# Dilated attention scores in 256-column products, taken 6 ticks later

## The chip, the cores and the metric

The kernel runs on one core of one Trainium2 chip. The metric is the device time of one execution in microseconds (us). Engines are named as in the profile: PE is TensorE (PEld its weight loads), DVE is VectorE, ACT is ScalarE, POOL is GpSimd, SP issues most of the DMAs.

## The reference

An encoder trunk of two layers over 512 tokens of 1024 features, in float32. Layer 0 is a gated linear recurrence, layer 1 is dilated sliding-window attention; each is followed by a gated feed-forward block with a width-3 convolution, with LayerNorms between. Only the scores of the attention are touched. There are 16 heads of 64 features and three groups of (window, dilation): (128, 1), (512, 4), (2048, 16). For each group, with keys gathered by stride:

```
s = einsum(q, k) * Dh**-0.5 - slope[h] * |distance|   # masked outside the window
p = exp(s - max(s));  o = einsum(p, v) / sum(p)
```

and the outputs of the three groups are merged by their softmax denominators, then projected by `w_o`.

## The kernel before, in words

**Products.** A float32 product is made from parts: each operand x is split into a rounded high part (ACT copies it to the type float32r) and the rest x - high (DVE subtracts), and a projection is three PE passes, high*high, high*low and low*high, accumulated in PSUM (`passes`, L216 to L219). Projection weights come by DMA as 128x1024 tiles (`wraw`), are split two units ahead of their use (ACT L156 makes `whi`, DVE L159 makes `wlo`), and are loaded four ahead.

**Order.** Everything is emitted in an order written out by the program; each engine then runs its own instructions in that order and waits by semaphores. The clock of that order is the *tick*: in a unit of a q or k projection (`cols_unit`, L278) one tick follows each of 8 steps of three 512-column matmuls; in a unit of the v projection (`v_unit`, L998) one follows every two steps, six 256-column matmuls. At a tick one item may be taken from two queues, `scores` first, then `values`, and the next one no sooner than `GAP` = 2 ticks later (L266 to L276). So the items of attention stand singly between blocks of projection matmuls.

**Attention.** `ORDER` (L688) runs through four blocks: q and k of head pairs p = 2c and p = 2c+1 (for each group g = 0, 1, 2 one q unit and one k unit, 48 ticks a pair), then v of both pairs (48 ticks). After each q or k unit `evac` (L761) takes the result out of PSUM. For keys it makes, for each of the two heads h of the pair, a high part `ka[:, h]` and a low part `kl[:, h]` on 64 partitions (ACT L785, DVE L789), and copies each by a DMA on SP to the other 64 partitions (L787, L791). The query tile holds q's high part on the head's 64 partitions and its low part on the other 64. So one matmul of the query tile with `ka[:, h]`, over all 128 partitions, gives q times the high keys, and one with `kl[:, h]` adds q times the low keys.

After the k unit of a group `push_scores` (L857) puts the scores of its two heads in the queue, to be taken no sooner than `SLAG` = 10 ticks later (for p = 0 by `XLAG`: 10, 11 and 14). Group 0 is four items `score0` (L808), each with four matmuls of 256 columns (two runs of 128 keys); groups 1 and 2 are two items each, `score12` (L833): for each of four classes r of tokens two matmuls of 128 columns into one PSUM bank, with `ka` and then with `kl` on top, L840 and L841; then one DVE instruction adds the distance bias over 512 columns, L842. With the last head of group 2 the softmax parts are joined by `merge` (L874): small steps at 8 to 28 ticks after, and from `T0` = 56 ticks after, the items of `values`: `pv_turn` (four transposes of the probabilities, L946, split by ACT L389 and DVE L390) and, at least `LAG` = 9 ticks behind its turn, `pv_prod` (L971, L974).

**End of the stage.** After the last v unit the output projection begins (L1084 on): one tick after every job of three matmuls, items of `values` at every tick, then the LayerNorm.

**Room.** PSUM is 8 banks and SBUF 40 slots of 4 KB per partition, both given out first-freed-first by `Arena` (L35); whoever takes one waits for its last user.

Of the kernel before, what the change touches and what calls it, by code (L numbers as in the profile page):

```python
# [11 lines left out]
F32R = mybir.dt.float32r  # L12
I32 = mybir.dt.int32
AF = mybir.ActivationFunctionType
OP = mybir.AluOpType
# [10 lines left out]


GAP, GAP_WO = 2, 1
SLAG, XLAG = 10, (10, 11, 14)
LAG, LAG_WO, VLAG, OLAG, T0 = 9, 4, 10, 4, 56  # L30
DEEP = 3
WIDE = 1
# [24 lines left out]
def encoder(ctx: ExitStack, tc: tile.TileContext, x, ln_g, ln_b, rg_w_in, rg_conv_w, rg_conv_b,  # L57
            rg_w_a, rg_b_a, rg_w_x, rg_b_x, rg_lam, rg_w_out, at_w_qkv, at_w_o, ff_w_up,
            ff_conv_w, ff_conv_b, ff_w_down, out):
    nc = tc.nc  # L60
# [14 lines left out]
    sb = Arena(ctx.enter_context(tc.tile_pool(name="slots", bufs=1)), NSLOT, "s")  # L75
    small = ctx.enter_context(tc.tile_pool(name="small", bufs=2))
    ps = Arena(ctx.enter_context(tc.tile_pool(name="ps", bufs=1, space=bass.MemoryType.PSUM)), 8, "b")
    ctx.enter_context(tc.manual_schedule())

    def bank(name):  # L80
        return ps.get([128, 512], F32, name)
# [4 lines left out]
    def f(ap):  # L86
        return ap.bitcast(F32)
# [662 lines left out]
    def attention(i0, d0, d12):  # L750
        slopes = [2.0 ** (-8.0 * (h + 1) / H) for h in range(H)]
        qk, P0, P12, V = {}, {}, {}, {}
        o32, ohl = {}, {}
        stats = {}
        def cls(b, lo=0, hi=128):

            return b[lo:hi].rearrange("p (j r) -> p r j", r=4)
# [3 lines left out]
        def evac(p, g, which, b):  # L761
            if which == "q":
                qa = sb.get([128, 2, 512], F32R, "q")
                if g == 0:
                    src = lambda lo, hi: b[lo:hi].rearrange("p (n i r) -> p n r i", n=4, r=4)
                    dst = lambda h, lo, hi: qa[lo:hi, h].rearrange("p (n r i) -> p n r i", n=4, r=4)
                else:
                    src = lambda lo, hi: cls(b, lo, hi)
                    dst = lambda h, lo, hi: qa[lo:hi, h].rearrange("p (r j) -> p r j", r=4)
                for h, a, z, o, oz in halves:  # L770
                    nc.scalar.activation(dst(h, a, z), src(a, z), AF.Copy)
                for h, a, z, o, oz in halves:
                    nc.vector.tensor_tensor(dst(h, o, oz), src(a, z), f(dst(h, a, z)), OP.subtract)
                qk[p, g, "q"] = qa
            else:
                ka = sb.get([128, 2, 512], F32R, "k")
                kl = sb.get([128, 2, 512], F32R, "kl")
                if g == 0:
                    src = lambda lo, hi: b[lo:hi]
                    dst = lambda t, lo, hi: t[lo:hi]  # L780
                else:
                    src = lambda lo, hi: cls(b, lo, hi)
                    dst = lambda t, lo, hi: t[lo:hi].rearrange("p (r j) -> p r j", r=4)
                for h, a, z, o, oz in halves:
                    nc.scalar.activation(dst(ka[:, h], a, z), src(a, z), AF.Copy)  # L785
                for h, a, z, o, oz in halves:
                    nc.sync.dma_start(f(ka[o:oz, h]), f(ka[a:z, h]))  # L787
                for h, a, z, o, oz in halves:
                    nc.vector.tensor_tensor(dst(kl[:, h], a, z), src(a, z), f(dst(ka[:, h], a, z)), OP.subtract)  # L789
                for h, a, z, o, oz in halves:  # L790
                    nc.sync.dma_start(f(kl[o:oz, h]), f(kl[a:z, h]))  # L791
                qk[p, g, "k"] = (ka, kl)
            ps.put(b)

        scores, values = deque(), deque()
# [6 lines left out]
        def keys(t, lo, hi, blk):  # L802

            st = {0: (0, 64), 3: (320, 64)}.get(blk, (128 * blk - 64, 128))
            s = t[lo:hi]
            return bass.AP(tensor=s.tensor, offset=s.offset + st[0], ap=[list(s.ap[0]), [st[1], 2], [1, 128]])

        def score0(p, h, half):  # L808
            qa, (ka, kl) = qk[p, 0, "q"], qk[p, 0, "k"]
            sl = -8.0 * slopes[2 * p + h]  # L810
            if half == 0:
                if h == 0:
                    stats[p] = small.tile([128, 2, 2, 2, 4], F32, name="stats", bufs=2)
                P0[p, h] = sb.get([128, 4, 256], F32, "P0")
            b = bank("s0")
            for z in range(2):
                blk = 2 * half + z
                o = b[:, 256 * z:256 * z + 256].rearrange("p (a c) -> p a c", a=2)
                js = slice(128 * blk, 128 * blk + 128)
                nc.tensor.matmul(o, qa[:, h, js], keys(ka[:, h], 0, 128, blk), start=True, stop=False)  # L820
                nc.tensor.matmul(o, qa[:, h, js], keys(kl[:, h], 0, 128, blk), start=False, stop=True)
            for z in range(2):
                blk = 2 * half + z
                nc.vector.scalar_tensor_tensor(
                    P0[p, h][:, blk, :], d0[:, (0, 1, 1, 2)[blk], :], sl, b[:, 256 * z:256 * z + 256],
                    op0=OP.mult, op1=OP.add)
            ps.put(b)
            if half:
                softmax(p, h, 0, P0[p, h])
                if h:  # L830
                    drop(p, 0)

        def score12(p, h, g):  # L833
            qa, (ka, kl) = qk[p, g, "q"], qk[p, g, "k"]
            if g == 1:
                P12[p, h] = sb.get([128, 4, 2, 128], F32, "P12")
            b = bank("s12")
            for r in range(4):
                c = slice(128 * r, 128 * r + 128)
                nc.tensor.matmul(b[:, c], qa[:, h, c], ka[:, h, c], start=True, stop=False)  # L840
                nc.tensor.matmul(b[:, c], qa[:, h, c], kl[:, h, c], start=False, stop=True)  # L841
            nc.vector.scalar_tensor_tensor(  # L842
                P12[p, h][:, :, g - 1, :], d12[:, g - 1:g, :].to_broadcast([128, 4, 128]), -8.0 * slopes[2 * p + h],
                b.rearrange("p (r c) -> p r c", r=4), op0=OP.mult, op1=OP.add)
            ps.put(b)
            if g == 2:
                softmax(p, h, 1, P12[p, h].rearrange("p r g c -> p r (g c)"))
            if h:
                drop(p, g)
                if g == 2:  # L850
                    merge(p)

        def drop(p, g):
            for t in (qk.pop((p, g, "q")),) + qk.pop((p, g, "k")):
                sb.put(t)

        def push_scores(p, g):  # L857
            ready = after(XLAG[g] if p == 0 else SLAG)
            for h in range(2):
                if g == 0:  # L860
                    for half in range(2):
                        scores.append((ready, lambda h=h, half=half: score0(p, h, half)))
                else:
                    scores.append((ready, lambda h=h: score12(p, h, g)))

        def softmax(p, h, w, P):
            st = stats[p]
            nc.vector.tensor_reduce(st[:, w, 0, h, :], P, axis=AX.X, op=OP.max, negate=True)
            nc.vector.tensor_scalar(st[:, w, 0, h, :], st[:, w, 0, h, :], 0.125, None, op0=OP.mult)  # L869
            for b in range(4):  # L870
                nc.scalar.activation(P[:, b, :], P[:, b, :], AF.Exp, bias=st[:, w, 0, h, b:b + 1], scale=0.125,  # L871
                                     accum_out=st[:, w, 1, h, b:b + 1])
# [172 lines left out]
        for kind, n in ORDER:  # L1045
            for g in (range(3) if kind == "qk" else VG):
                if kind == "qk":
                    for which in "qk":
                        if n == 0 and g < 2:
                            if g == 0 and which == "q":  # L1050
                                fb = first_units(i, 4, ["q", "k", "q", "k"])
                                wrap()
                            b = fb.pop(0)
                        else:
                            b = bank("qk")
                            cols_unit(b, i)
                        evac(n, g, which, b)
                        i += 1
                    push_scores(n, g)
                else:  # L1060
                    while values and values[0][2] // 2 < n:
                        tick()
                    if n:
                        for z in range(2):
                            sb.put(V[g, z])
                    v_unit(n, g, i)
                    i += 2
                    if g == VG[-1]:
                        vdone[0] = n
                        vtime[0] = clock[0] + VLAG  # L1070
# [21 lines left out]
        while left or at_k.get(KD - 1, BIG) > clock[0]:  # L1092
# [9 lines left out]
            if job:  # L1102
                h, k, t = job
# [53 lines left out]
    d0, d12 = dist  # L1157
# [31 lines left out]
```

## Time and profile before

| | |
|---|---|
| Time, median of 3 runs | 1565.41 us (1564.68 to 1566.1) |
| The profiled execution's own time | 1563.55 us |
| its span, first to last instruction | 1561.8 us |
| PE busy | 1528.5 us (98%) |
| PEld busy | 1314.0 us (84%) |
| DVE busy | 920.1 us (59%) |
| ACT busy | 662.2 us (42%) |
| POOL busy | 145.8 us (9%) |
| mean granted TensorE clock | 0.996 |

Busy is the time in which at least one instruction of the engine was under way; PE's ends are modelled and its matmuls overlap, so PE's pace is read from the starts of its instructions. The chain of waits goes back from the last instruction, at each step to what released it. All times inside the execution are us from the span's start; the attention stage lies between about 612 and 1177 us.

### The profile page before, as it was taken

The page shows a single profiled execution, that of the slowest core. Times are in us where ns is not written, and L with a number is a line of the kernel's source. Part 1 is how long each engine was busy: PE and PEld are TensorE (multiplying, and loading weights), DVE is VectorE, ACT ScalarE, POOL GpSimd, SP SyncE. Part 2 cuts the span into 40 slices and gives each one's busy share as a digit, 9 for nine tenths or more (in the row PEclk, how much of TensorE's full clock was granted, in tenths as well). Part 3 has the DMA queues.
Part 4 walks back from the last instruction along what each step waited for, and adds up shares of the span by engine and source line. Part 5 has one row for each costly group of instructions (what it writes and reads, how often), then busy time and mean ns, then how long its engine had stood idle before and what let it go on. Part 6 is the DMA issues. An engine that isn't in the chain of part 4 may idle for free.

```text
span 1561.8 us, 20972 instructions
## 1 busy us (share of the span) xinstructions
PE 1528.5 (98%) x8115; PEld 1314.0 (84%) x8115; DVE 920.1 (59%) x1314; ACT 662.2 (42%) x1062; POOL 145.8 (9%) x367
## 2 busy tenths in 40 slices
PE   7899999999999999999999999999999999999998
PEld 6678889888888888979889889988988888888886
DVE  5688786564544245685677668568657445454225
ACT  3678942333333211554455455355542433333210
POOL 2211002000000002022012001101202000000001
PEclk9999999999999999999999999999999999999999
DMA  5956643222323331335343343433434222323311
GB/s 174 202 131 131 207 147 95 81 82 83 89 85 121 121 108 54 85 106 162 82 116 123 100 122 103 141 94 110 148 115 129 82 81 87 88 81 108 135 68 54
DMA packets 228752, 173.04 MB, mean 111 GB/s; under 512 B 17294, under 2 KB 205996, under 8 KB 228652
## 3 DMA queue, kind: packets, MB, share of 16 engines
q1 hardware_dynamic: 210860, 159.11, 33.8%
q0 software_dynamic: 17792, 12.58, 3.7%
q8 instruction: 64, 1.05, 0.3%
q14 instruction: 36, 0.29, 0.1%
HBM read 145.44 MB, written 2.10 MB: 94 GB/s over the span
## 4 chain that ended last, share of the span: by engine, by line
PE 90%; DVE 4%; DMA 2%; ACT 2%; issue 1%; POOL 1%; SPq 0%; DVEq 0%; ACTq 0%; POOLq 0%
PE v L218 24%; PE o L218 20%; PE g L218 15%; PE qk L218 15%; PE gate L218 2%; PE u L218 2%; PE gb L218 2%; PE tP L946 2%; PE oT L974 1%; PE oT L971 1%; PE s L841 1%; PE s L840 1%; PE q L218 1%; PE k L218 1%; PE tx L326 1%
## 5 line engine op out<-in xcount | busy, mean ns | idle before, releaser
L159 DVE TENSOR_TENSOR wlo<-wraw,whi 128x1024 fp32r<-128x1024 f32 x247 | 300.0, 1224 | 225.8 <-ACT whi L156 190.1
L156 ACT ACTIVATE whi<-wraw 128x1024 fp32r<-128x1024 f32 x236 | 245.3, 1052 | 111.5 <-PE o L218 102.9
L218 PE MATMUL o<-whi,h 128*128 128x512 f32 x704 | 217.4, 389 | 0.0
L218 PEld LDWEIGHTS o<-whi,h 128*128 128x128 f32 x704 | 132.1, 188 | 27.4
L218 PE MATMUL qk<-xhi,whi 128*128 128x512 f32 x352 | 145.3, 413 | 0.0
L218 PE MATMUL g<-xlo,whi 128*128 128x512 f32 (+1 forms) x384 | 142.8, 372 | 1.6 <-DVE xlo L330 1.6
L218 PE MATMUL g<-xhi,whi 128*128 128x512 f32 (+1 forms) x384 | 142.8, 372 | 0.3 <-ACT xhi L329 0.2
L218 PE MATMUL v<-xhi,whi 128*128 128x512 f32 (+1 forms) x384 | 142.7, 372 | 0.0
L218 PE MATMUL g<-xhi,wlo 128*128 128x512 f32 (+1 forms) x384 | 142.6, 371 | 0.0
L218 PE MATMUL v<-xhi,wlo 128*128 128x512 f32 (+1 forms) x384 | 142.6, 371 | 0.0
L218 PE MATMUL v<-xlo,whi 128*128 128x512 f32 (+1 forms) x384 | 142.6, 371 | 0.0
L218 PE MATMUL qk<-xlo,whi 128*128 128x512 f32 x352 | 138.2, 393 | 0.0
L218 PE MATMUL qk<-xhi,wlo 128*128 128x512 f32 x352 | 137.9, 392 | 0.0
L218 PE MATMUL o<-wlo,h 128*128 128x512 f32 x352 | 136.9, 389 | 0.0
L218 PE MATMUL v<-whi,xhi 128*128 128x256 f32 x352 | 101.2, 288 | 0.0
L218 PE MATMUL v<-whi,xlo 128*128 128x256 f32 x352 | 99.7, 283 | 0.0
L218 PE MATMUL v<-wlo,xhi 128*128 128x256 f32 x352 | 99.6, 283 | 0.0
L401 DVE SCALAR_TENSOR_TENSOR t<-g,fft,t 128x511 f32<-128x511 f32 x44 | 33.0, 750 | 109.8 <-ACT t L399 109.6
L871 ACT ACTIVATE P<-P,stats 128x256 f32<-128x256 f32 x128 | 63.6, 498 | 78.8 <-DVE stats L869 78.8
L399 ACT ACTIVATE t<-g,fft 128x512 f32<-128x512 f32 x44 | 34.4, 781 | 130.9 <-PE g L218 130.8
L218 PEld LDWEIGHTS g<-xlo,whi 128*128 128x128 f32 x384 | 72.4, 188 | 14.3 <-DVE xlo L330 2.0
L218 PEld LDWEIGHTS g<-xhi,whi 128*128 128x128 f32 x384 | 72.4, 189 | 13.3 <-ACT xhi L329 0.8
(201 smaller groups left out, 3080.7 us busy)
## 6 DMA issues: line engine op xcount, KB each, us to landing
wraw<-in_ff_w_up_dram SPq DMA_DIRECT2D x88, 512.0 KB
wraw<-in_at_w_qkv_dram SPq DMA_DIRECT2D x72, 512.0 KB
wraw<-in_ff_w_down_dram SPq DMA_DIRECT2D x44, 512.0 KB
wraw<-in_rg_w_in_dram SPq DMA_DIRECT2D x20, 512.0 KB
whi<-in_rg_w_in_dram POOLq DMA_DIRECT2D x16, 512.0 KB, 5.6
V<-vst SPq DMA_DIRECT2D x128, 64.0 KB
k<-k SPq DMA_DIRECT2D x48, 128.0 KB
kl<-kl SPq DMA_DIRECT2D x48, 128.0 KB
```

What stands on the lines that cost most here:

```text
L156: nc.scalar.activation(hi, raw, AF.Copy)
L159: (nc.gpsimd if pool else nc.vector).tensor_tensor(lo, raw, f(hi), OP.subtract)
L218: nc.tensor.matmul(o, lhs[a], rhs[b], start=start and n == 0, stop=stop and n == 2, skip_group_check=skip)
L326: nc.tensor.transpose(b[:, 128 * k:128 * k + 128], xt[t][:, 128 * (4 * q + k):128 * (4 * q + k) + 128], ident)
L399: nc.scalar.activation(t1, bg, AF.Identity, bias=tab[:, 3 * NF + fi:3 * NF + fi + 1], scale=tab[:, NF + fi:NF + fi + 1])
L401: nc.vector.scalar_tensor_tensor(t1[:, 1:], bg[:, :511], tab[:, fi:fi + 1], t1[:, 1:], op0=OP.mult, op1=OP.add)
L840: nc.tensor.matmul(b[:, c], qa[:, h, c], ka[:, h, c], start=True, stop=False)
L841: nc.tensor.matmul(b[:, c], qa[:, h, c], kl[:, h, c], start=False, stop=True)
L871: nc.scalar.activation(P[:, b, :], P[:, b, :], AF.Exp, bias=st[:, w, 0, h, b:b + 1], scale=0.125, accum_out=st[:, w, 1, h, b:b + 1])
L946: nc.tensor.transpose(tb[:, 128 * n:128 * n + 128], a, ident)
L971: nc.tensor.matmul(ov0, v(0, s), pt[:, n, 0:256].rearrange("p (b r i) -> p r b i", b=2, r=4), start=(s == 0 and n == 0), stop=False, skip_ ...
L974: nc.tensor.matmul(ov[:, s, :], v(g, s), pt[:, n, 128 + 128 * g:256 + 128 * g], start=False, stop=(s == 3 and n == 1 and g == 2), skip_gro ...
```

## The change

Per head, the high and the low keys of a group now lie side by side in one tile `kk[h]` (index 0 high, 1 low). In `score12` one matmul of 256 columns takes both, so that q times high keys and q times low keys come out next to each other instead of on top of each other; two PSUM banks instead of one hold the result, and DVE adds the halves: for each bank one instruction for the bias and the high half and one that adds the low half. `score0` and the copies keep their work with the new tiles. `SLAG` and `XLAG` grow by 6 ticks.

```diff
-SLAG, XLAG = 10, (10, 11, 14)
+SLAG, XLAG = 16, (16, 17, 20)
...
-                ka = sb.get([128, 2, 512], F32R, "k")
-                kl = sb.get([128, 2, 512], F32R, "kl")
+                kk = [sb.get([128, 2, 512], F32R, "k") for h in range(2)]
...
                 for h, a, z, o, oz in halves:
-                    nc.scalar.activation(dst(ka[:, h], a, z), src(a, z), AF.Copy)
+                    nc.scalar.activation(dst(kk[h][:, 0], a, z), src(a, z), AF.Copy)
                 for h, a, z, o, oz in halves:
-                    nc.sync.dma_start(f(ka[o:oz, h]), f(ka[a:z, h]))
+                    nc.sync.dma_start(f(kk[h][o:oz, 0]), f(kk[h][a:z, 0]))
                 for h, a, z, o, oz in halves:
-                    nc.vector.tensor_tensor(dst(kl[:, h], a, z), src(a, z), f(dst(ka[:, h], a, z)), OP.subtract)
+                    nc.vector.tensor_tensor(dst(kk[h][:, 1], a, z), src(a, z), f(dst(kk[h][:, 0], a, z)), OP.subtract)
                 for h, a, z, o, oz in halves:
-                    nc.sync.dma_start(f(kl[o:oz, h]), f(kl[a:z, h]))
-                qk[p, g, "k"] = (ka, kl)
+                    nc.sync.dma_start(f(kk[h][o:oz, 1]), f(kk[h][a:z, 1]))
+                qk[p, g, "k"] = kk
...
-                nc.tensor.matmul(o, qa[:, h, js], keys(ka[:, h], 0, 128, blk), start=True, stop=False)
-                nc.tensor.matmul(o, qa[:, h, js], keys(kl[:, h], 0, 128, blk), start=False, stop=True)
+                nc.tensor.matmul(o, qa[:, h, js], keys(kk[:, 0], 0, 128, blk), start=True, stop=False)
+                nc.tensor.matmul(o, qa[:, h, js], keys(kk[:, 1], 0, 128, blk), start=False, stop=True)
...
-            b = bank("s12")
+            bs = [bank("s12") for _ in range(2)]
+            bv = [b.rearrange("p (r z c) -> p r z c", r=2, z=2) for b in bs]
             for r in range(4):
                 c = slice(128 * r, 128 * r + 128)
-                nc.tensor.matmul(b[:, c], qa[:, h, c], ka[:, h, c], start=True, stop=False)
-                nc.tensor.matmul(b[:, c], qa[:, h, c], kl[:, h, c], start=False, stop=True)
-            nc.vector.scalar_tensor_tensor(
-                P12[p, h][:, :, g - 1, :], d12[:, g - 1:g, :].to_broadcast([128, 4, 128]), -8.0 * slopes[2 * p + h],
-                b.rearrange("p (r c) -> p r c", r=4), op0=OP.mult, op1=OP.add)
-            ps.put(b)
+                nc.tensor.matmul(bv[r // 2][:, r % 2], qa[:, h, c], kk[:, :, c], start=True, stop=True)
+            for n in range(2):
+                o = P12[p, h][:, 2 * n:2 * n + 2, g - 1, :]
+                nc.vector.scalar_tensor_tensor(o, d12[:, g - 1:g, :].to_broadcast([128, 2, 128]),
+                                               -8.0 * slopes[2 * p + h], bv[n][:, :, 0, :], op0=OP.mult, op1=OP.add)
+                nc.vector.tensor_tensor(o, o, bv[n][:, :, 1, :], OP.add)
+                ps.put(bs[n])
```

## Rows read from the trace of the kernel before

**Rows 1.** Page: busy us per engine; the chain by engine.
```profile
PE 1528.5 (98%) x8115; PEld 1314.0 (84%) x8115; DVE 920.1 (59%) x1314; ACT 662.2 (42%) x1062; POOL 145.8 (9%) x367
...
PE 90%; DVE 4%; DMA 2%; ACT 2%; issue 1%; POOL 1%; SPq 0%; DVEq 0%; ACTq 0%; POOLq 0%
```

**Rows 2.** Busy by stretch: PE, PEld, DVE, ACT, POOL (us), clock, DMA share, GB/s.
```profile
735.00:835.00 100.00, 100.00 (x584) 87.12 (x583) 68.70 (x116) 51.32 (x106) 6.80 (x32) 1.00 0.37 105
835.00:880.00 45.00, 45.00 (x331) 42.67 (x331) 25.67 (x55) 19.70 (x44) 8.73 (x32) 1.00 0.37 115
```

**Rows 3.** Groups by line: xcount | busy us, mean ns | idle before.
```profile
L841 PE MATMUL s<-kl,q 128*128 128x128 f32 x128 | 30.3, 276 | 1.1 <-DVE R L897 1.1
...
L840 PE MATMUL s<-k,q 128*128 128x128 f32 x128 | 28.7, 262 | 0.5 <-DMA k<-k 0.5
```

**Rows 4.** Chain of waits, score12 between q/k matmuls: start us, us, what.
```profile
691.63 1.42 PE qk L218 x6
693.05 0.06 PE s L840
693.11 0.11 PE s L841
...
693.89 2.83 PE qk L218 x12
```

**Rows 5.** Chain of waits, a score0 item (four products) and what follows.
```profile
807.54 0.12 PE s L820
...
808.01 1.39 PE qk L218 x6
```

**Rows 6.** One line, PEld of the score products: duration ns min/median/max.
```profile
L840 PEld LDWEIGHTS s<-k,q x128: 186/192/192, 653.7 to 1096.4; 128*128 128x128 f32 x128
```

**Rows 7.** Groups by line, VectorE and one of ACT.
```profile
L390 DVE TENSOR_TENSOR pt<-tP,pt 128x512 fp32r<-128x512 f32 x64 | 43.4, 688 | 42.8 <-ACT pt L389 41.9
...
L389 ACT ACTIVATE pt<-tP 128x512 fp32r<-128x512 f32 x64 | 37.8, 598 | 61.8 <-PE tP L946 52.8 <-DMA V<-vst 6.0 <-issue 2.2
...
L824 DVE SCALAR_TENSOR_TENSOR P<-d,s 128x256 f32<-128x256 f32 x64 | 23.0, 414 | 0.2
...
L842 DVE SCALAR_TENSOR_TENSOR P<-d,s 128x512 f32<-128x512 f32 x32 | 21.3, 685 | 6.2 <-PE s L841 5.9
...
L1027 DVE TENSOR_TENSOR vst<-v,vst 128x256 fp32r<-128x256 f32 x32 | 13.0, 419 | 13.5 <-ACT vst L1026 13.4
```

**Rows 8.** DVE timeline at the end of a q/k phase: start us, us, instruction.
```profile
825.06 1.14 DVE L910 TENSOR_SCALAR P<-P,sc 128x256 f32<-128x256 f32 x4
826.22 0.69 DVE L982 TENSOR_TENSOR o<-oT,ot 64x512 f32<-64x512 f32 x1
826.94 1.29 DVE L842 SCALAR_TENSOR_TENSOR P<-d,s 128x512 f32<-128x512 f32 x2
```

**Rows 9.** Chain of waits there, the matmuls behind the first item.
```profile
822.25 1.45 PE qk L218 x6
```

**Rows 10.** Timeline around two waits of PE: start us, us, instruction [idle before <-releaser].
```profile
673.64 0.39 PE L218 MATMUL qk<-xhi,wlo 128*128 128x512 f32 x1
...
674.48 0.36 PE L820 MATMUL s<-k,q 128*128 128x256 f32 x1 [0.45 <-DMA k<-k]
...
675.78 0.36 PE L821 MATMUL s<-kl,q 128*128 128x256 f32 x1 [0.95 <-DMA kl<-kl]
...
688.38 0.39 PE L218 MATMUL qk<-xhi,wlo 128*128 128x512 f32 x1
...
689.25 0.30 PE L840 MATMUL s<-k,q 128*128 128x128 f32 x1 [0.48 <-DMA k<-k]
...
690.66 0.30 PE L841 MATMUL s<-kl,q 128*128 128x128 f32 x1 [1.12 <-DVE R L897]
```

**Rows 11.** Chain of waits at the stage's end: the last three products, then ACT.
```profile
1165.72 0.12 PE oT L971
...
1167.76 0.60 ACT ot L981
```

More of the change, by code (lines that the diff above doesn't have):

```diff
@@ L808, in score0 @@
         def score0(p, h, half):
-            qa, (ka, kl) = qk[p, 0, "q"], qk[p, 0, "k"]
+            qa, kk = qk[p, 0, "q"], qk[p, 0, "k"][h]
             sl = -8.0 * slopes[2 * p + h]
@@ L833, in score12 @@
         def score12(p, h, g):
-            qa, (ka, kl) = qk[p, g, "q"], qk[p, g, "k"]
+            qa, kk = qk[p, g, "q"], qk[p, g, "k"][h]
             if g == 1:
                 P12[p, h] = sb.get([128, 4, 2, 128], F32, "P12")
-            b = bank("s12")
+            bs = [bank("s12") for _ in range(2)]
+            bv = [b.rearrange("p (r z c) -> p r z c", r=2, z=2) for b in bs]
             for r in range(4):
                 c = slice(128 * r, 128 * r + 128)
-                nc.tensor.matmul(b[:, c], qa[:, h, c], ka[:, h, c], start=True, stop=False)
-                nc.tensor.matmul(b[:, c], qa[:, h, c], kl[:, h, c], start=False, stop=True)
-            nc.vector.scalar_tensor_tensor(
-                P12[p, h][:, :, g - 1, :], d12[:, g - 1:g, :].to_broadcast([128, 4, 128]), -8.0 * slopes[2 * p + h],
-                b.rearrange("p (r c) -> p r c", r=4), op0=OP.mult, op1=OP.add)
-            ps.put(b)
+                nc.tensor.matmul(bv[r // 2][:, r % 2], qa[:, h, c], kk[:, :, c], start=True, stop=True)
[5 more added lines that the diff above has]
+                ps.put(bs[n])
             if g == 2:
@@ L853, in drop @@
         def drop(p, g):
-            for t in (qk.pop((p, g, "q")),) + qk.pop((p, g, "k")):
+            for t in [qk.pop((p, g, "q"))] + qk.pop((p, g, "k")):
                 sb.put(t)
```

## The prediction

> **What bounds the kernel now.** I read the page's busy times and its chain first. PE is busy for 1528.5 of 1561.8 us and carries 90% of the chain that ended last; DVE carries 4% and is busy 59% [rows 1]. So a microsecond of PE's work that goes from the attention stage is a microsecond of the time, as long as no other engine comes late instead. An average over the kernel says nothing of this stage, so the next view is the busy time by stretch. From 735 to 835 us (most of the q and k units of pairs 2 and 3) PE has no gap and DVE is busy 68.70 us of 100; from 835 to 880 us (most of the v unit behind them) DVE is busy 25.67 of 45; the granted clock is 1.00, the full 2.4 GHz, in both [rows 2]. DVE is the engine to watch, since the change takes work from PE and gives work to it. Then come the chain in order of time around single score items, which shows PE's pace by starts (its durations are modelled), and the few places where PE waits.
>
> **Part 1: eight products of 128 columns become four of 256.** There are 128 matmuls each at L840 and L841, that is 32 items of eight [rows 3]. One item starts at 693.05 and the projection goes on at 693.89: 0.84 us, in which each step after the first takes 0.11 [rows 4]. Six projection matmuls take 1.42 us behind such an item, but 1.39 behind an item of 256-column products [rows 4, 5]; these 0.03 us are a tail of the narrow products. Together 0.87 us. For the new product `score0` is the same in shape, the same kind of query weights and a moving operand of two runs of 128 keys: it steps by 0.12 us, and four products take 0.47 us, from 807.54 to 808.01, with no tail [rows 5]. So an item should fall from 0.87 to 0.47 us. From starts elsewhere I read differences of 0.39 to 0.43, and take 0.41. Times 32: 13.1 us off PE (12.5 to 13.8). What is saved is per instruction: 1024 columns an item stream as before, but the weight loads, 0.19 us each [rows 6], are halved in number.
>
> The Trainium skill (TensorE: Matmul & The Clock Gate, section Back-to-back issue gap) lists an isolated gap of 134 cycles at 128 columns and 262 at 256, nearly in proportion to the columns, and says itself that this under-counts narrow products in streams that load weights each time. By that table eight gaps would be an estimated 0.45 us and four 0.44, and the edit would save an estimated 0.3 us in all. The trace has 0.11 and 0.12 us, far from a ratio of two [rows 4, 5], so I go by the rows and keep the table's case as a rival.
>
> **Part 2: DVE adds the halves.** One instruction of 512 columns, 0.685 us, becomes four of 256: two that add the bias to what is in PSUM, 0.414 us each by L824, and two plain additions with one operand in PSUM, for which the nearest row is L1027, 0.419 us [rows 7]. That is 1.67 us, 0.98 more an item and 31.4 us more in all; the order of L824 and L1027 is so close that I put no more than 2 us of the 31.4 in doubt.
>
> What hides it is DVE's idle time, and the lag decides where it falls. Group 1 of an odd pair was taken 10 ticks after its push, which is 6 before the v unit begins; it is now taken at the v unit's first tick. So the q/k phase of two pairs holds four items instead of six, and the v phase four instead of two. DVE's sum in the q/k phase goes from 68.70 us to 68.7 - 6 x 0.685 + 4 x 1.67 = 71.3 of some 97; in the v phase from 25.67 to 25.67 - 2 x 0.685 + 4 x 1.67 = 31.0 of 44 [rows 2, 7]. Both are about 72%, so DVE isn't the bound on average. The tight place is the end of the q/k phase, where it works without a break and comes only at 826.94 to the two items of the odd pair's group 1 [rows 8], though PE had left the first at 822.25 [rows 9]. Just these two leave that place. If that cover fails, all of 31.4 us can come out on PE.
>
> Behind DVE's new instructions wait the low parts of weights, of turned probabilities and of keys, and the banks: an item now takes two of 8. Counting the takings through the order, with 0.69 us a tick, 0.47 an item of scores and 0.44 to 0.62 one of values (estimates from the pieces of the chain), a bank comes round again no sooner than 8.8 us after its last writer before the change, and 6.9 after. In the tight place DVE is done with a bank 5 to 6 us after PE [rows 8, 9]; with an extra 1 us ahead of it that is 6 to 7, just at the limit. I put 1.5 us of new waits into the sum, with bounds of 0 and 9 (up to 3 us in each of the three later pairs of pairs).
>
> **Part 3: 6 ticks more between keys and scores.** PE waits for scores in two places, both in pair 1. A `score0` started 0.84 us after the matmul ahead of it, where a projection step takes 0.23, and its low-key product 1.30 us later where 0.12 is due; a `score12` 0.87 for 0.23 and then 1.41 for 0.11 [rows 10]. What is lost is 1.79 and 1.94, 3.7 us together, behind the DMAs of `k` and `kl`. Six ticks are 4.1 us of projection, more than either wait, so both go. The new product needs the low keys from its first matmul on; they are what the longer half of each wait was for, and the same lag covers them. The DMAs keep their number, size and place on SP, and start later only by DVE's backlog. The bounds are 0 and 3.7.
>
> The lag has a price at the stage's end. The last pair's merge comes 6 ticks later and its turns 4 later (they stand behind pair 6's, which keep their ticks). The projection's jobs run out at the same tick as before, so the last two turns and their products lose the jobs between them. The last turn then has only three products ahead of its own, 2.0 us in the rows [rows 11], against 0.598 + 0.688 us for splitting its result [rows 7]; it fits unless ACT's 0.60 us for the first head [rows 11] stands in front. That is 0 to 1.5 us, and I take 0.7. The four spare jobs that cover the last head's evacuation are there as before. Slots: keys take two as before, kept 6 ticks longer; loads of weights go out four units, about 22 us, ahead, so I cost it at nothing. Without that cover it would be a wait of the size of part 3's, 2 us.
>
> **Sum.** 1563.55 - 13.1 - 3.7 + 1.5 + 0.7 = 1549.0 for the profiled execution. The median of the runs lies 1.9 us above it, so I forecast 1551 us, with its own range from 1547 (13.8 and 3.7 saved and nothing paid: 1547.9, and a little for what isn't seen) to 1555 (12.5 and 3.7 saved, 5.5 paid: 1554.7).
>
> **Rivals.**
> *DVE's backlog takes part back.* The additions meet turns, scale factors and weights; a late `pt`, `wlo` or bank stops PE for 6 to 12 us in all. For it: DVE works without a break at the end of each q/k phase [rows 8]. Against: the lag moves work out of that place. 1565.4 - 16.8 + 0.7 and 6 to 12 on it: 1555 to 1561. Chance 0.15.
> *DVE becomes the bound, slower than before.* If each added microsecond of DVE comes out on PE, 31.4 us come back: 1565.4 - 16.8 + 31.4 = 1580. Its place is the bank that is taken again before DVE has emptied it; it decides from the point where DVE's delay stays above 6.9 us. Against: 72% busy in both phases. Chance 0.06.
> *The pace follows the columns.* Four products of 256 columns last as long as eight of 128, and only the waits go: 1565.4 - 3.7 + 0.7 + 1.5 = 1564. Against: rows 4 and 5. This is the table's case. Chance 0.03.
> *The two waits stay*, because they hang on something that moves along with the lag: 1551 + 3.7 = 1554.7. Chance 0.04.
>
> **How the numbers follow.** The forecast has 0.72. The range 1546 to 1560 holds it, the case of the waits and most of DVE's partial case; it leaves out the slower case, that of the columns and the tails of the others, some 0.15. 0.2% or 3.1 us is about what a measurement of this kernel can tell from no change, so faster is below 1562.3. Faster: 0.72 + 0.04 + 0.13 = 0.89; same: 0.02 + 0.03 = 0.05; slower: 0.06.
>
> **What would show it.** In the changed kernel the score products of the two groups should be 128 at 0.12 us from start to start, with about 0.47 us from an item's start to the next projection matmul; in pair 1 no gap ahead of `s`; DVE's bias instructions of these groups 64 of 0.41 us, and 64 additions of 0.42; the stretch from the first scores to the projection some 15 us shorter. The prediction is wrong if an item still takes over 0.8 us, or if gaps of PE ahead of `pt`, `wlo` or the first product in a bank sum to over 6 us.

## The result and the profile after

The changed kernel took 1589.11 us (median of 4 runs, 1587.88 to 1591.66) against 1565.05 us before on the same chip: a ratio of 1.0153, 95% interval 1.014 to 1.0167. It is 24 us slower; 1551 us were forecast, with a range that ended at 1560.

Page of the changed kernel: busy time of the engines, and the chain by engine, in answer to [rows 1].

```profile
PE 1533.5 (97%) x7987; PEld 1314.1 (83%) x7987; DVE 946.1 (60%) x1410; ACT 658.9 (42%) x1062; POOL 127.7 (8%) x367
...
PE 34%; DVE 8%; ACT 3%; issue 2%; SPq 0%; POOL 0%; DMA 0%; DVEq 0%; ACTq 0%; POOLq 0%
```

PE is busy 5 us longer with 128 instructions fewer. The two chains can't be set side by side, 34% against 90%: the second was followed back only to about 820 us, and its parts add up to some 48% of the span. Within what it covers PE has about seven tenths and DVE, ACT and issue gaps most of the rest, so the chain does leave PE more often than before.

Busy by stretch over the attention stage (columns as in [rows 2]), first of the kernel before, then of the changed one.

```profile
612.00:1191.00 579.00, 572.45 (x3662) 513.92 (x3660) 395.88 (x702) 282.33 (x588) 81.79 (x268) 1.00 0.39 114
```

```profile
612.00:1217.00 605.00, 577.21 (x3537) 513.94 (x3535) 422.19 (x798) 279.02 (x588) 63.43 (x268) 0.97 0.38 110
```

The whole loss is in this stage, 26 us longer. PE sits idle 27.8 us in it (605 - 577.2), where it was 6.6: 21 us more. And the granted clock, which was 1.00, is 0.97 on average. Over the span the mean is 0.984 for 0.996, which is 25.4 us of full speed not granted (0.016 x 1587.8) where it was 6.2; so 19 us more, of which some fell into idle time. The balance fits: 26 us longer, with 21 of idle time more and 13 of products less (the forecast saving, which the rows below bear out), leaves 18 for the slower PE.

The products and the additions themselves came out as forecast. PE timeline of the changed kernel around an item (start us, us), which answers to [rows 4, 5]:

```profile
780.46 0.39 PE L218 MATMUL qk<-xhi,wlo 128*128 128x512 f32 x1
780.69 0.64 PE L841 MATMUL s<-k,q 128*128 128x256 f32 x4
781.16 0.40 PE L218 MATMUL qk<-xhi,whi 128*128 128x512 f32 x1
```

Groups by line, answering to [rows 7]:

```profile
L846 DVE TENSOR_TENSOR P<-P,s 128x256 f32<-128x256 f32 x64 | 26.9, 421 | 2.2
L844 DVE SCALAR_TENSOR_TENSOR P<-d,s 128x256 f32<-128x256 f32 x64 | 26.6, 416 | 7.7 <-PE s L841 7.1
```

An item takes 0.47 us from its first start to the next projection matmul, and DVE's four instructions 0.416 and 0.421 us each, 1.67 in all.

So where does PE wait? The changed kernel's waits of PE from 640 to 1180 us, the largest first (us in total, times, longest):

```profile
PE v L218 <- DVE vst L1029: 7.0, 3, 2.4
PE oT L973 <- ACT pt L389: 4.9, 3, 1.6
PE v L218 <- DVE wlo L159: 4.7, 4, 1.2
PE v L218 <- ACT whi L156: 3.6, 1, 3.6
PE o L218 <- DVE ohl L996: 3.1, 1, 3.1
```

The second of these, which comes once in each of the three later blocks of two pairs, in the timeline of the changed kernel, all engines:

```profile
801.89 0.60 PE L948 MATMUL tP<-ident,P 128*128 128x128 f32 x4
...
804.99 0.42 DVE L846 TENSOR_TENSOR P<-P,s 128x256 f32<-128x256 f32 x1
...
805.45 1.22 DVE L870 TENSOR_REDUCE stats<-P 128x4 f32<-128x1024 f32 x1
806.70 0.17 DVE L871 TENSOR_SCALAR stats<-stats 128x4 f32<-128x4 f32 x1
806.90 0.51 ACT L873 ACTIVATE P<-P,stats 128x256 f32<-128x256 f32 x1 [4.80 <-DVE stats L871]
...
809.01 0.60 ACT L389 ACTIVATE pt<-tP 128x512 fp32r<-128x512 f32 x1
...
809.66 0.38 PE L973 MATMUL oT<-pt,V 128*128 128x256 f32 x1 [1.63 <-ACT pt L389]
```

Read it upwards. PE waits for turned probabilities `pt`. ACT has idled 4.80 us, though the transposes that it copies were issued at 801.89: the copy `pt` stands in its order behind four exponentials of a softmax, and the first of them waits for the maximum from DVE. DVE gets to that maximum only after the score work ahead of it. What is late is not an engine that has too much to do, but an order in which ACT's copies stand behind exponentials, and these behind DVE.

The largest of the waits, at the first product of a block's last v unit, that of group 0, is the same order once more. PE needs a bank out of which ACT and then DVE have to take an earlier v result (`vst`), and ACT's copy stands behind four exponentials that wait for a maximum:

```profile
855.70 0.51 ACT L873 ACTIVATE P<-P,stats 128x256 f32<-128x256 f32 x1 [4.51 <-DVE stats L871]
...
857.68 0.63 ACT L1028 ACTIVATE vst<-v 128x256 fp32r<-128x256 f32 x2
...
858.55 0.52 PE L218 MATMUL v<-whi,ends 128*128 128x256 f32 x1 [2.35 <-DVE vst L1029]
```

The waits for `whi` and `wlo` stand at the entry of the v units; e1 below shows them in detail.

What comes after such a wait can cost as much again. PE timeline of the changed kernel behind the wait for `pt`, and the busy time of that stretch (column before the DMA share: granted clock):

```profile
811.64 0.63 PE L218 MATMUL qk<-xhi,wlo 128*128 128x512 f32 x1
812.07 0.63 PE L218 MATMUL qk<-xhi,whi 128*128 128x512 f32 x1
```

```profile
806.00:813.50 7.50, 5.70 (x25) 4.39 (x24) 4.27 (x8) 5.99 (x14) 2.95 (x16) 0.82 0.22 79
```

The matmuls start 0.43 us apart instead of 0.23, the pace of the lower level, 1.2 GHz, for some 3 us.

The last place is the stage's end. DVE's timeline and PE's there, changed kernel:

```profile
1146.48 1.13 DVE L909 TENSOR_SCALAR P<-P,ss 128x256 f32<-128x256 f32 x4
1147.53 1.13 DVE L912 TENSOR_SCALAR P<-P,sc 128x256 f32<-128x256 f32 x4
...
1148.92 2.01 DVE L996 TENSOR_TENSOR ohl<-o,ohl 128x512 fp32r<-128x512 f32 x2
```

```profile
1146.50 0.40 PE L218 MATMUL o<-wlo,ohl 128*128 128x512 f32 x1
1150.00 1.22 PE L218 MATMUL o<-whi,ohl 128*128 128x512 f32 x2 [3.10 <-DVE ohl L996]
```

The last pair's scale steps (L909, L912), 6 ticks later than before, now stand on DVE right ahead of the projection's first operand `ohl`.

### The profile page after: what moved, and what is told of

It is laid out like the page before. It is cut to its first block, busy times and chain, and to the rows that moved or that the text cites. A ratio compares the mean times of both kernels' runs of the same rounds, so it can differ in the third digit from the quotient of the medians.

```text
span 1587.8 us, 20828 instructions
## 1 busy us (share of the span) xinstructions
PE 1533.5 (97%) x7987; PEld 1314.1 (83%) x7987; DVE 946.1 (60%) x1410; ACT 658.9 (42%) x1062; POOL 127.7 (8%) x367
```

## The experiments

Ratios are to the kernel before, run on the same chip (1565.6, 1566.7 and 1565.9 us in the three sets). 128 and 256 are the columns of a `score12` product, and DVE an item is in us. The three sets ran on three chips. Waits are read from one profiled execution of each run; in e3 and e6 it took 4 and 5.5 us more than the median.

| run | products | DVE an item | lag | else | us | ratio (95%) |
|---|---|---|---|---|---|---|
| e1 | 128 | 0.685 | 16 | | 1576.93 | 1.0075 (1.0054 to 1.0097) |
| e2 | 256 | 1.67 | 10 | | 1571.90 | 1.0041 (1.0026 to 1.0056) |
| e3 | 256 | 0.83 | 16 | | 1571.30 | 1.0043 (1.0026 to 1.0059) |
| e4 | 128 | 1.67 | 10 | | 1573.24 | 1.0052 (1.0034 to 1.0071) |
| e5 | 256 | 1.67 | 13 | | 1585.88 | 1.0126 (1.0111 to 1.0141) |
| e6 | 128 | 0.685 | 13 | | 1577.81 | 1.0081 (1.0062 to 1.01) |
| e7 | 256 | 0.83 | 10 | | 1556.97 | 0.9943 (0.9928 to 0.9958) |
| e8 | 256 | 1.67 | 16 | scale later | 1584.28 | 1.0117 (1.01 to 1.0134) |
| e9 | 256 | 1.67 | 10 | exponentials later | 1550.29 | 0.9899 (0.9883 to 0.9916) |
| e10 | 128 | 0.685 | 10 | exponentials later | 1558.90 | 0.9959 (0.9944 to 0.9974) |
| e11 | 256 | 1.67 | 16 | both later | 1548.68 | 0.9892 (0.9878 to 0.9907) |
| e12 | 256 | 1.67 | 10 | exponentials later, scale on GpSimd | 1547.24 | 0.9887 (0.9873 to 0.9902) |

### First set: which part of the change costs the time

**e1**, the kernel before with the new lags.

```diff
-SLAG, XLAG = 10, (10, 11, 14)
+SLAG, XLAG = 16, (16, 17, 20)
```

> The kernel before with the lags of the changed one (16; 16, 17, 20) and nothing else. Theory A (the length of the DVE additions: they stretch the alternation of ACT and DVE until PE waits) expects the two waits in pair 1 to go and nothing to come, 1560 to 1564 us, no gap above 1 us on PE between 640 and 1140 us. Theory B (the lag itself: scores now fall on the tick at which a unit ends, ahead of the evacuation of the next keys or values on ACT and DVE) expects most of the loss here: 1575 to 1587 us, with a lowered clock behind gaps as in the changed kernel.

1576.93 us: the lag alone costs 11 us, as theory B said in kind. The waits in pair 1 are gone, but at the entry of each v unit after the first there is a new one. ACT's timeline, then PE's, of e1:

```profile
820.68 0.51 ACT L871 ACTIVATE P<-P,stats 128x256 f32<-128x256 f32 x1 [1.51 <-DVE stats L869]
...
823.27 1.19 ACT L771 ACTIVATE q<-qk 64x512 fp32r<-64x512 f32 x2
824.49 1.06 ACT L156 ACTIVATE whi<-wraw 128x1024 fp32r<-128x1024 f32 x1
```

```profile
825.59 0.38 PE L218 MATMUL v<-whi,xhi 128*128 128x256 f32 x1 [0.92 <-ACT whi L156]
827.20 0.58 PE L218 MATMUL v<-wlo,xhi 128*128 128x256 f32 x1 [1.22 <-DVE wlo L159]
827.57 0.42 PE L218 MATMUL v<-whi,xlo 128*128 128x256 f32 x1
827.79 0.41 PE L218 MATMUL v<-whi,xhi 128*128 128x256 f32 x1
```

Again ACT's copies (queries, then the weights that PE wants) stand behind the exponentials of group 0, which wait for DVE; then DVE's low part comes late in turn. The steps that follow are 0.22 us where 0.12 is due. At the stage's end PE waits 2.8 us for `ohl`.

**e2**, the changed kernel with the old lags (the diff above, reversed).

> The changed kernel with the old lags (10; 10, 11, 14): 256-column products and additions on DVE alone. Theory A expects it slow like the changed kernel, 1575 to 1595 us, since DVE's work is the same and the odd pair's group 1 is back in the tight end of the q/k phase. Theory B expects PE's 13.1 us to come through, with the two waits of pair 1 still there: 1550 to 1556 us.

1571.90: neither theory's number. PE's 13 us don't show, and the walls are other ones. Timeline of e2 in pair 1, all engines:

```profile
670.67 1.22 DVE L870 TENSOR_REDUCE stats<-P 128x4 f32<-128x1024 f32 x1
...
672.13 0.51 ACT L873 ACTIVATE P<-P,stats 128x256 f32<-128x256 f32 x1 [0.94 <-DVE stats L871]
...
674.23 1.21 ACT L784 ACTIVATE k<-qk 64x512 fp32r<-64x512 f32 x2
...
676.18 1.19 SPq L790 DMA_DIRECT2D k<-k  x2
...
677.20 0.55 PE L819 MATMUL s<-k,q 128*128 128x256 f32 x1 [5.82 <-DMA k<-k]
```

The copy of the keys waits on ACT behind the exponentials, so their DMA starts late and PE waits 5.8 us, then 2.5 us at the next scores, and about 2 us in each later v unit.

**e3**, the changed kernel without the addition of the low half.

```diff
-                nc.vector.tensor_tensor(o, o, bv[n][:, :, 1, :], OP.add)
```

> The changed kernel without the addition of the low half (the scores of groups 1 and 2 leave out query times low keys): products, two banks and lag 16 stay, DVE has 0.83 us an item instead of 1.67. Theory A expects the gaps to go: 1547 to 1555 us. Theory B and a theory C (two PSUM banks an item make PE wait for a bank) expect it to stay above 1572 us.

1571.30: 18 us less than the changed kernel, so DVE's length matters, but not as far as theory A said, and the time lies just under what B and C asked for. The waits at the entry of the v units and at the stage's end (4.3 us) stay. The 7.0 us for a bank behind `vst` are gone although an item still takes two banks, so the second bank by itself, theory C's cause, doesn't make them.

**e4**, the kernel before with DVE's work of the changed one.

```diff
-            nc.vector.scalar_tensor_tensor(
-                P12[p, h][:, :, g - 1, :], d12[:, g - 1:g, :].to_broadcast([128, 4, 128]), -8.0 * slopes[2 * p + h],
-                b.rearrange("p (r c) -> p r c", r=4), op0=OP.mult, op1=OP.add)
+            bv = b.rearrange("p (n r c) -> p n r c", n=2, r=2)
+            for n in range(2):
+                o = P12[p, h][:, 2 * n:2 * n + 2, g - 1, :]
+                nc.vector.scalar_tensor_tensor(o, d12[:, g - 1:g, :].to_broadcast([128, 2, 128]),
+                                               -8.0 * slopes[2 * p + h], bv[:, n], op0=OP.mult, op1=OP.add)
+                nc.vector.tensor_tensor(o, o, bv[:, n], OP.min)
```

> The kernel before (128-column products, one bank, lag 10) with DVE's work an item as in the changed kernel: two bias instructions of 256 columns and two more instructions of the same shape that take the smaller of sum and product, which changes no value. Theory A expects it slower than before by at least the changed kernel's new waits and lost clock, 1590 to 1620 us, since nothing is saved on PE. Theory B expects 1565 to 1570 us; so does theory C.

1573.24: DVE's length costs 7.6 us by itself, far from the 31 us that it adds, mostly in the two places of pair 1 (4.1 and 0.8 us at the first, where it was 0.5 and 0.9). Lag and length each cost 8 to 11 us alone; together, with PE's saving, 24.

### Second set: a lag between, and the pieces of each wall

**e5**, the changed kernel with lags 13; 13, 14, 17, and **e6**, the kernel before with them.

```diff
+SLAG, XLAG = 13, (13, 14, 17)
```

> The changed kernel with lags between (13; 13, 14, 17). Theory F (two walls: with lag 10 the long DVE work makes keys late for the scores, with 16 the scores' softmax holds ACT and DVE at the entry of the v unit and the scale steps hold DVE ahead of the projection's operands; between them there is room) expects a good part of PE's 13 us to come through: 1553 to 1563 us. Rival G (DVE's additions cost their time at any lag) expects 1568 us or more.

> The kernel before with lags 13; 13, 14, 17 and nothing else. Theory F expects the two waits for keys in pair 1 (3.7 us) to go and no wait at the entry of the v units above 0.5 us: 1560 to 1564 us. If already 3 ticks more bring the walls of lag 16, 1567 us or more.

1585.88 and 1577.81: there is no room between. e5 has both kinds of waits (5.8 us for keys in pair 1, about 1.3 and 1.2 us at each later v entry) and a new one, 1.3 us behind DVE's part of a query, in each of the three later blocks; and e6 has nearly all of e1's. Theory F fell.

**e7**, e2 without the low addition.

> The changed kernel with the old lags and without the addition of the low half (scores of groups 1 and 2 leave out query times low keys). Theory H (with lag 10 the loss is DVE's length, which makes the next keys late) expects the waits for keys to shrink to those of the kernel before, 3.7 us, and PE's 13 us to come through: 1551 to 1555 us. Rival I (the new product needs the low keys at its first matmul, and waits for their DMA whatever DVE does) expects waits of 5 us and more in pair 1 and 2 us at each v unit to stay: 1560 us or more.

1556.97, 9.7 us faster than before. With the old lag and a short DVE the 256-column products pay, though pair 1 still waits 2.2 + 0.9 us for keys and 1.9 us at its next scores, which the profile puts down to a small DVE step of the merge. Theory H's direction holds; its waits were a little longer and its time 2 us too low.

**e8**, the changed kernel with the scale steps 8 ticks later.

```diff
-            for dt, fn in ((8, gather), (14, joint_max), (18, joint_sum), (24, lambda: scale(0, 0)),
-                           (25, lambda: scale(0, 1)), (27, lambda: scale(1, 0)), (28, lambda: scale(1, 1))):
+            for dt, fn in ((8, gather), (14, joint_max), (18, joint_sum), (32, lambda: scale(0, 0)),
+                           (33, lambda: scale(0, 1)), (35, lambda: scale(1, 0)), (36, lambda: scale(1, 1))):
```

> The changed kernel with the four scale steps of the softmax 8 ticks later (32 to 36 after the merge instead of 24 to 28). If the scale steps, moved by the lag to the end of the v unit, hold DVE ahead of the projection's first operands, PE's wait of 3.3 us there and the lowered clock after it go: 5 to 6 us less than the changed kernel, 1582 to 1585 us; the waits at the entry of the v units stay, since the softmax of group 0 makes them. If the scale steps also make those, 1575 us or less.

1584.28, 4.8 us less than the changed kernel (6.4 when each is taken against the kernel before that ran beside it), and at the stage's end PE's timeline in e8 reads

```profile
1146.42 0.73 PE L218 MATMUL o<-whi,ohl 128*128 128x512 f32 x2 [0.37 <-DVE ohl L996]
```

0.37 us for 3.10. So the scale steps made that wait, and no other.

### Third set: ACT's order

The rows so far put the exponentials ahead of copies that PE needs. In **e9** (on e2), **e10** (on the kernel before) and **e11** (on e8) they are emitted 7 ticks after their maximum, with the same work.

```diff
-            for b in range(4):
-                nc.scalar.activation(P[:, b, :], P[:, b, :], AF.Exp, bias=st[:, w, 0, h, b:b + 1], scale=0.125,
-                                     accum_out=st[:, w, 1, h, b:b + 1])
+            def exps():
+                for b in range(4):
+                    nc.scalar.activation(P[:, b, :], P[:, b, :], AF.Exp, bias=st[:, w, 0, h, b:b + 1], scale=0.125,
+                                         accum_out=st[:, w, 1, h, b:b + 1])
+
+            at_tick(clock[0] + 7, exps)
```

> The changed kernel with the old lags, and the four exponentials of each softmax emitted 7 ticks after its maximum, so that on ACT the copies of the next keys, queries and weights stand ahead of them. Theory J (the loss comes through ACT's order: copies wait behind exponentials, which wait for DVE's longer work) expects the waits for keys in pair 1 (8 us and the lowered clock) mostly to go and PE's 13 us to show: 1552 to 1562 us. Rival K (DVE's own length makes the keys' low parts late, ACT's order doesn't matter) expects 1568 us or more.

> The kernel before with the exponentials 7 ticks later and nothing else. Theory J expects the two waits for keys in pair 1 (3.7 us) to shrink: 1561 to 1564 us. Rival K expects 1565 to 1567 us, no change.

> The changed kernel with its lags, the scale steps 8 ticks later and the exponentials 7 ticks later. Theory J expects the waits at the entry of the v units (whi, then wlo) and for turned probabilities behind ACT to go too: 1553 to 1565 us. Rival K expects 1578 us or more.

1550.29, 1558.90 and 1548.68. Theory J holds in direction in all three, and each is some 2 to 4 us faster than its range: from e2 to e9 about 21.6 us go, and from e8 to e11 about 35.6 us, by nothing but the place of the exponentials in ACT's order. The same place as in e2, in the timeline of e9:

```profile
667.79 1.21 ACT L784 ACTIVATE k<-qk 64x512 fp32r<-64x512 f32 x2 [2.87 <-PE qk L218]
...
671.26 1.22 DVE L870 TENSOR_REDUCE stats<-P 128x4 f32<-128x1024 f32 x1
...
673.29 1.19 SPq L790 DMA_DIRECT2D k<-k  x2
...
675.61 0.35 PE L820 MATMUL s<-k,q 128*128 128x256 f32 x1 [0.45 <-DMA k<-k]
```

The keys' copy no longer waits for the maximum, and 0.45 us is left of the wait. In e10 both waits of pair 1 are gone at the old lag, so they too hung on ACT's order. What PE still waits for in e11, from 640 to 1180 us (us in total, times, longest), and the busy time of its stage:

```profile
PE o L218 <- ACT ohl L999: 1.5, 1, 1.5
PE g L218 <- DVE xlo L330: 1.2, 1, 1.2
PE o L218 <- DVE ohl L1000: 0.8, 2, 0.4
PE oT L977 <- DVE pt L390: 0.7, 1, 0.7
```

```profile
612.00:1178.00 566.00, 561.03 (x3544) 503.12 (x3543) 424.17 (x801) 280.65 (x589) 68.46 (x269) 1.00 0.40 118
```

DVE is busy 424 us of 566 there, more densely than in the changed kernel (422 of 605), and PE is idle for 5 us at a mean clock of 1.00.

**e12**, e9 with the scale steps on GpSimd.

```diff
-                        nc.vector.tensor_scalar(P0[p, h][:, b, :], P0[p, h][:, b, :], ss[:, 0, h, b:b + 1], None, op0=OP.mult)
+                        nc.gpsimd.tensor_scalar(P0[p, h][:, b, :], P0[p, h][:, b, :], ss[:, 0, h, b:b + 1], None, op0=OP.mult)
...
-                        nc.vector.tensor_scalar(pv, pv, sc[:, h, b:b + 1], None, op0=OP.mult)
+                        nc.gpsimd.tensor_scalar(pv, pv, sc[:, h, b:b + 1], None, op0=OP.mult)
```

> The changed kernel with the old lags, the exponentials 7 ticks later, and the scale steps on GpSimd instead of DVE, which takes 16 x 0.347 = 5.6 us a pair off DVE. If what is then left is DVE's length (theory K in part), 3 to 8 us less than the same kernel with scale steps on DVE. If GpSimd is slow enough to make the turns late, more than that kernel.

1547.24, 3 us under e9 at the edge of what was expected, but the intervals overlap, so it isn't shown that 5.6 us a pair off DVE help. A scale step takes 1.0 to 1.1 us on GpSimd, where DVE took 0.35, and none of PE's waits in the stage names GpSimd. e9, e11 and e12 beat both kernels; which of them is best stays open.

## Why the prediction was wrong

**Part 1 held.** An item takes 0.47 us, and with the new waits away the saving is there. The stage's first projection matmul and the first of the output projection, in e10 and then in e11:

```profile
613.66 0.39 PE L218 MATMUL q<-xhi,whi 128*128 128x256 f32 x1 [0.25 <-ACT xhi L329]
1121.65 0.50 PE L218 MATMUL o<-whi,ohl 128*128 128x512 f32 x1 [1.49 <-ACT ohl L997]
```

```profile
614.33 0.39 PE L218 MATMUL q<-xhi,whi 128*128 128x256 f32 x1 [0.25 <-ACT xhi L329]
1108.92 0.50 PE L218 MATMUL o<-whi,ohl 128*128 128x512 f32 x1 [1.49 <-ACT ohl L999]
```

That is 508.0 us with narrow products and 494.6 with wide ones, 13.4 less; e9's stretch is 496.5, of which 1.3 are waits for keys. The forecast was 13.1. The medians differ by less, 8.6 us from e10 to e9 and 10.2 to e11, for reasons outside the products, as far as these executions show them: e9's came to the stage 3.2 us later, through work that the edit doesn't touch, and e11's took 2.2 us longer behind the projection's start, with 0.70 us of wait for `pt` and matmuls at the lower clock for some 2.5 us.

**Part 2 failed at one step: "Both are about 72%, so DVE isn't the bound on average", and from it 1.5 us of new waits, with bounds of 0 and 9.** PE's idle time grew by 21 us instead. The price of the additions was right (1.67 us), and DVE was indeed not short of time: e11 has the same additions in a shorter stage. But I listed what is queued behind DVE's new instructions without following it through the next engine. The maximum on DVE releases four exponentials on ACT, and behind these stand ACT's copies of keys, queries, weights, v results and turned probabilities. DVE's work ahead of the maximum can delay them all, though ACT is idle. The page of before held the hint in a row that I passed over. Moving the exponentials took 7 us off that kernel too (e10, by the medians; its trace shows 3.9 of them up to the output projection). ACT's exponentials in the groups by line (xcount | busy, mean ns | idle before, releaser), before and after:

```profile
L871 ACT ACTIVATE P<-P,stats 128x256 f32<-128x256 f32 x128 | 63.6, 498 | 78.8 <-DVE stats L869 78.8
```

```profile
L873 ACT ACTIVATE P<-P,stats 128x256 f32<-128x256 f32 x128 | 63.6, 498 | 119.9 <-DVE stats L871 116.0
```

The last column is ACT standing still ahead of exponentials, 41 us longer than before; in the places shown above, the copy that PE needed stood right behind them.

**Part 3 had its sign wrong.** The two waits in pair 1 went, as forecast; but the lag was not what they needed, since e10 loses them at the old one. Nor do the rows put all of them down to DMAs, as I did: for the longest the releaser is a DVE step of the merge, L897 [rows 10]. And to charge the lag with only 0.7 us, at the end, was wrong: 6 ticks move the softmax too. The lag alone costs 11 us (e1) where 3.0 were to be won. By e1's rows the exponentials of group 0 land ahead of the copies for the v unit, and the scale steps ahead of the projection's operands (2.8 us of wait; 3.1 in the changed kernel, and e8 shows that the scale steps make it). For the first of these the test is e11, in the changed kernel; e1 with later exponentials wasn't run. I took the late tick of an odd pair's scores for relief, counted DVE's sums, and left out ACT.

**The clock had no term.** The rows of before show 1.00, and I priced a wait by its own length. By the balance above about 18 us are matmuls at the lower level, so that 21 us of new idle time cost nearly 40.

**The rivals.** "DVE's backlog takes part back" named late `pt` and `wlo`, which is what the rows show, but as DVE's own lateness and at 6 to 12 us. The slower rival came nearest in time, 1580 us, but not by its reason: DVE's 31 us don't come out on PE, only 7.6 do (e4). Its place, a bank that isn't empty yet, is there, in the 2.4 us behind `vst` in each of the three later blocks. But that bank is v's, and it is late because ACT's copy stands behind exponentials; the wait is gone in e11 with DVE's work unchanged. The rival in which the pace follows the columns, with no saving in the products, is refuted by the 0.47 us an item and by the stretches of e9 and e11.

## What to carry to other kernels

A mean busy share says whether an engine has room, not whether it hands over in time: follow each lengthened instruction to what it releases, and then to all that stands behind that on the second engine's in-order queue. Where copies that feed the bounding engine stand behind work that waits for a third engine, move the waiting work later in the order before shortening anything; here this was worth 22 and 36 us in the changed kernel at the two lags and 7 in the kernel before, beside some 13 from the products. And when a delay is lengthened to cover one wait, list every later step that moves along with it and what it then stands ahead of.

## What the runs showed of the hardware

That a wait of PE costs more than its length was not expected at this size: behind a wait of 1.63 us and one of 0.17 us, 512-column matmuls started 0.43 us apart instead of 0.23 for some 3 us, and behind 3.10 us in the projection from 1150 to 1155. A single wait of 1.22 us at 830 us of the changed kernel was followed by matmuls at full pace from the second on. The length of a wait doesn't decide it alone: at the start of the output projection e10 and e11 have the same two waits, 1.49 and 0.37 us, and behind them 512-column matmuls start 0.23 us apart in e10, but 0.43 apart for some 2.5 us in e11.
